# Mixer of a macaron block on one core: modulation sums tied to marked chain steps, w_out's first pieces taken into the last group's stage, sigmoid written with tanh

## The chip, the core and the metric

The kernel runs on one core of one Trainium2 chip. The metric is the device time of one execution in microseconds (us). PE is the matrix engine (PEld its weight loads), DVE the vector engine, ACT the scalar engine, POOL the GpSimd engine, and SP the engine whose queue starts most of the DMAs. Each engine works through its own instructions in order; they wait for one another by semaphores.

## The reference

One transformer block in float32 on x of 256 rows by 2048 columns. Three sublayers stand one behind the other: a SwiGLU feed-forward (ffn1), a mixer, and a second feed-forward (ffn2), each with a norm before and behind it. Nine vectors of 2048 modulate them (shift, scale and gate of each sublayer); they are c's silu times a matrix of 2048 x 18432, plus a bias.

```python
mod = (silu(c) @ w_ada + b_ada).reshape(3, 3, D)
x = x + w * (1 + gate) * rms_norm(fn(modulate(rms_norm(x, pre), shift, scale)), post)   # three times
# fn of the mixer:
p = h @ w_in                       # 512 pool columns, then r, k, v (1536 each), then 64 + 64 + 224
y_pool = multiscale_pool(p[:, :512])          # windows 2, 4, 8, 16, then a 128x128 product each
y_rwkv = rwkv7_time_mix(p[:, 512:])           # 24 heads of 64, a recurrence over the 256 rows
out = concatenate([y_pool, y_rwkv]) @ w_out
```

In rwkv7_time_mix the gate is `sigmoid(xg) @ g2`, where xg are the last 224 columns after a token shift. The recurrence carries a 64 x 64 state per head.

## The kernel before, in words

**Products.** Each weight is split into a rounded part hi (on ACT, line 185) and a rest lo (on DVE, line 186), each activation likewise, and a product is three matmuls. Line 201 issues nearly all matmuls. The dense work of the mixer comes in pieces: `dense` (line 796) makes 256 columns of w_in with two 1 MB loads and eight pieces of 12 matmuls, and yields after each; `rows_pieces` (line 588) does the same for w_out, whose pieces are six matmuls of 512 columns for one k-tile and one column block (two halves of the rows). Raw weights have two buffers, split ones four.

**Mixer.** `mixer` (line 818) begins with `outer`, which norms and modulates the input k-block by k-block and multiplies it at once with the lora columns and with r, k and v of the first head group. `lora` (line 845) then shifts the small columns; two of its three parts go through Sigmoid, the first through Tanh, and `use_ln_exp` loads the table for exp and ln behind them. Six groups of two 128-column pairs follow. A group's recurrence is done in chunks of 64 rows by two generators:

- `rwkv_a` (line 1035) has seven segments: decay and gates; the scaled keys and queries (its DVE work ends with bk, ar and wc, lines 1092 to 1103); the bonus and v; two of chunk products G; T1 and the diagonal blocks (to dg, line 1147); and the inverse of the 8 x 8 blocks, a chain of 14 small DVE steps on xt and x (lines 1166 and 1168) that ends with Z1, Z0 (the transpose of line 1175).
- `rwkv_b` (line 1178) has thirteen: four for the doubling of the inverse (pm, Z), two for its lower half (pm at line 1245, X), the corrections, three state steps S (line 1287), the output y (sq), its norm (sb<-t, the rsqrt) and the gate product (sb<-xg), which writes two k-tiles of yT.

`stage` (line 888) writes one group's order out: twelve slots; in each slot two pieces of dense work, then one segment of the old b, of b, and, in seven of the slots (0, 2, 4, 5, 6, 7, 9), of a. Each PE instruction is tied to the one before (`ordered`, line 192), so this order is PE's order until `ordered` is cleared. The dense pieces of stages 0 to 4 are the next group's r, k and v, 24 of them. Stage 5 has the 16 pieces of the pool columns, used up by slot 7; its slots 8 to 11 hold the pool's window sums and two of its four products. A last stage without a runs b of group 5, beside 24 of the 32 pieces of w_out's first two column blocks; the last k-tiles (14 and 15) come from that b, so eight pieces stand behind it. `late` (line 940) splits finished k-tiles of yT into hT, the input of w_out, whose buffer was w_in's input. Then come w_out's third and fourth column block, with `post_rows` behind each block.

**Modulation in the mixer.** `ada_run` (line 273) works off the rest of four groups of sums: vector 5, then three parts of vectors 7 and 6 (two of 2 x 256 columns, one of 2 x 512). Loads of 512 KB go into four places in x's buffer, which is saved to DRAM for that time (line 884) and read back when all is done (line 934). A load's sum is one DVE operation of 1024 elements per partition, or two of 512 (lines 255 and 257). All four groups use one accumulator tile, `acc`. When a group's 2048 rows are summed, its matmuls (`ada_mod`, line 310) and the DVE operation at line 322 follow in one of the slots 1, 3, 8, 10, 11. `stage` calls `ada_run` at the end of a slot, 0.8 times per slot while a runs; three calls only load, each group takes two calls beside its sums.

**Order on the engines other than PE.** The program gives the dependences and a priority (the order in which it is written, moved ahead for some operations), and a list scheduler fixes each engine's order before the run: an operation that is ready may be put ahead of an earlier one that isn't. `later` (line 335) ties an operation behind `self.urgent`, if that lies on its engine: the sums pass through it, and line 1028. In the mixer of before, `urgent` is last set in `outer`.

Of the kernel before, what the change touches and what calls it, by code (L numbers as in the profile page):

```python
# [11 lines left out]
F32 = mybir.dt.float32  # L12
# [5 lines left out]
P = 128  # L18
T = 256
# [13 lines left out]
ADA_FFN1, ADA_MIXER, ADA_OUT, ADA_FFN2 = 2.8, 0.8, 3, 12  # L33
# [48 lines left out]
class Block:  # L82
# [190 lines left out]
    def ada_run(self, upto, places):  # L273
# [162 lines left out]
    def post_begin(self, s, weight, more, psum, rows, junk):  # L436

        nc = self.nc
# [6 lines left out]
        ps = self.tile(psum, [P, 512], tag="mm")  # L445
        nc.tensor.transpose(ps[:KD, :P], g, self.ident)
# [137 lines left out]
    def rows_block(self, *args, **kw):  # L584
        for _ in self.rows_pieces(*args, **kw):
            pass

    def rows_pieces(self, load, nkt, per, x, banks, apart, done, more=(), warm=None, wide=1, order=None):
# [5 lines left out]
        parts = ((0, 0, 512), (1, 0, 256), (1, 256, 256)) if apart else [  # L594
            (tt, 512 * h, 512) for h in range(wide) for tt in range(2)]
        held = []

        def use(b, k0, hi, lo):
            tt, c0, n = parts[b]
            cs = slice(c0 % 512, c0 % 512 + n)  # L600
            for k in range(per):
                kt = k0 + k
                self.rows_mm(banks[b][:, :n], tt, hi[:, k, cs], lo[:, k, cs], x(kt), kt == ends[0], kt == ends[1])

        order = order or range(nkt // 4 * wide)
        ends = 4 // wide * order[0], 4 // wide * (order[-1] + 1) - 1
        for kc in order:
            raw = load(kc)
            for pc in range(0, 4 // wide, per):
                k0 = 4 // wide * kc + pc  # L610
                if wide > 1:
                    for h in range(wide):
                        hi, lo = self.split(raw[:, pc:pc + per, 512 * h:512 * h + 512])
                        for b in (2 * h, 2 * h + 1):
                            use(b, k0, hi, lo)
                        yield
                    continue
# [195 lines left out]
    def tick(self):  # L813
        self.chunks += 1
        if int(self.chunks / self.every) > int((self.chunks - 1) / self.every) and self.ada_pos < self.ada_end[ADA_AHEAD]:
            self.ada_step(self.mm)

    def mixer(self, ctx):
        nc, tc, I = self.nc, self.tc, self.I
        pool = lambda name, bufs, **kw: ctx.enter_context(tc.tile_pool(name=name, bufs=bufs, **kw))  # L820
        self.chunks, self.every = 0, ADA_MIXER
# [23 lines left out]
        def lora(i, ps):  # L845
            if i == 0:
                self.shift(xa, ps, "mu_shift", 36)
                last.append(nc.scalar.activation(xw[:C, :], xa[:C, :], AF.Tanh))
            else:
                key, j = (("mu_shift", 37), ("mu_tail", 0))[i - 1]  # L850
                t = self.tile(self.w2p, [P, T], tag="t1")
                self.shift(t, ps, key, j)
                last.append(nc.scalar.activation(xg[:, i - 1, :], t, AF.Sigmoid))
# [56 lines left out]
        us = {}  # L910

        def pool_weights():
            for h in range(2):
                yield from self.dense(w_in, h * 2 * P, 2, self.hT, lambda i, ps: us.__setitem__(2 * h + i, ps))
# [3 lines left out]
        for g in range(n):  # L918
            state[g] = {}
            a = self.rwkv_a(state[g], g, *(rkv[g, w] for w in range(3)))  # L920
            pieces = weights(g + 1) if g < n - 1 else pool_weights()
            tasks = {}
# [4 lines left out]
            stage(a, b, b_old, pieces, tasks)  # L927
            b, b_old = self.rwkv_b(g, state[g]), b
            for run in (pieces, a):
                for _ in run:  # L930
                    pass
# [3 lines left out]
        rows = self.tile(self.gp, [P, 2, 1024], tag="G")  # L935
        junk = self.tile(self.w2p, [P, 2, 512], tag="bt")
        self.post_begin(1, 1.0, True, self.mm, [rows[:, h, :] for h in range(2)], [junk[:, i, :] for i in range(2)])
        row = lambda t: self.tile(self.mm if t == "mm" else self.pa, [P, 512], tag=t)

        def late(ks):  # L940
            for k in ks:
                y = self.yT[:, k, :]
                nc.scalar.copy(self.hT[:, k, 0, :], y)
                nc.vector.tensor_tensor(self.hT[:, k, 1, :], y, self.hT[:, k, 0, :].bitcast(F32), ALU.subtract)

        self.split_ahead = 300
        self.every = ADA_OUT
        for q, tags in ((0, ("mm", "mm", "sa", "ga")), (2, ("pb", "zb")), (3, ("sb", "y", "mm"))):
            banks = [row(t) for t in tags]
            w = 2 if q == 0 else 1  # L950

            def load(kc):
                raw = self.load(I["w_out"], 4 // w * kc, 4 // w, q * 512, w * 512)
                if not self.ordered:
                    self.tick()
                return raw

            def done(tt, c0, n, ps):
                self.post_rows(q + c0 // 512, tt, c0 % 512, n, ps)
# [3 lines left out]
            order = [2, 3, 4, 5, 6, 0, 1, 7] if q == 0 else None  # L963
            pieces = self.rows_pieces(load, KD, 1, lambda k: self.hT[:, k], banks, q == 3, done, more, self.mm, w, order)
            if q == 0:
# [4 lines left out]
                for _ in b:  # L970
                    pass
                late((14, 15))
                self.ordered, self.pe_last = False, None
            for _ in pieces:
                pass

    def pool_begin(self, us):

        nc = self.nc
        self.pool_w = [self.tile(self.w2p, [P, 2, P], tag=t, bufs=1) for t in ("lw2", "la2")]  # L980
        for i, w in enumerate(self.pool_w):
            nc.sync.dma_start(w, self.I["pool_w"][2 * i:2 * i + 2].rearrange("i p c -> p i c"))
        work = self.tile(self.w2p, [P, 6 * T], tag="bk", bufs=1)
        more = self.tile(self.w2p, [P, 2 * T], tag="T1")
        n = PAD + T
        self.pool_u = work[:, :4 * n].rearrange("p (i t) -> p i t", i=4)
        self.pool_s = [work[:, 4 * n:5 * n], more[:, :n]]
        for t in [self.pool_u[:, :, :PAD]] + [s[:, :PAD] for s in self.pool_s]:
            nc.vector.memset(t, 0.0)
        for i in range(4):  # L990
# [454 lines left out]
```

## Time and profile before

| what | value |
|---|---|
| median of 3 runs | 2153.83 us (2153.71 to 2160.31) |
| the profiled execution's own time | 2149.33 us |
| its span, first to last instruction | 2147.5 us |
| mean granted clock of PE | 0.982 |
| mixer's opening, to the first a-segment | 795 to 889.9 us of the span |
| stages 0 to 5 | 889.9 to 1265.8 us |
| last stage and w_out | 1265.8 to 1372 us |

Times inside the profile count from the first instruction. A line of the timeline gives start, length, engine, line of the program, operation, output<-inputs, shape and count, and in brackets the idle time before it and what ended that. A row of a table by stretches gives from:to and length, each engine's busy time with its count of instructions, then PE's granted clock (1.00 is full), the DMA engines' busy share and GB/s. In a row of the waits stand total, number and longest. PE counts as busy while matmuls are queued one behind the other, also at half clock.

### The profile page before, as it was taken

What the parts mean: (1) busy time and instruction counts of PE and PEld (TensorE: products, weight loads), DVE (VectorE), ACT (ScalarE), POOL (GpSimd) and SP (SyncE); (2) the same over time, 40 slices, a digit from 0 to 9 for tenths busy, and PEclk for the clock granted to TensorE, in tenths of its full rate; (3) what the DMA queues carried; (4) which work ended last, traced back from release to release, by engine and by line L of the source; (5) the groups of instructions that cost most, each with busy time, mean ns of one, the idle gap of its engine ahead of it and who ended that gap; (6) DMA issues with size and microseconds to landing.
All of it is one profiled execution on the core that took longest, in us unless ns stands there. A gap on an engine that the chain in (4) does not pass through costs nothing.

```text
span 2147.5 us, 38718 instructions
## 1 busy us (share of the span) xinstructions
PE 2052.9 (96%) x15987; PEld 1825.8 (85%) x15987; DVE 1595.1 (74%) x2204; ACT 1023.3 (48%) x1503; POOL 0.2 (0%) x4
## 2 busy tenths in 40 slices
PE   3999999999999998899998999999999999999998
PEld 3999988888888887799887877899998888888886
DVE  6798898788887777777888675778899455555556
ACT  3534543444434556655444545653454344443453
POOL 0000000000000000000000000000000000000000
PEclk8999999999999998999998999999999999999999
DMA  9999888999888837843655334598887555555553
GB/s 313 359 313 329 276 284 323 313 322 319 303 325 298 284 113 242 258 124 109 180 160 190 102 105 140 212 345 284 315 296 252 196 193 181 194 182 193 194 190 124
DMA packets 313711, 506.62 MB, mean 236 GB/s; under 512 B 13013, under 2 KB 173886, under 8 KB 313022
## 3 DMA queue, kind: packets, MB, share of 16 engines
q1 hardware_dynamic: 312044, 500.78, 68.7%
q10 hardware_dynamic: 1490, 3.36, 0.5%
q8 instruction: 125, 2.05, 0.4%
q14 instruction: 52, 0.43, 0.1%
HBM read 499.87 MB, written 4.22 MB: 235 GB/s over the span
## 4 chain that ended last, share of the span: by engine, by line
PE 86%; DVE 6%; DMA 4%; ACT 3%; issue 2%; SPq 0%; DVEq 0%; ACTq 0%
PE mm L201 50%; PE mm L212 16%; PE mm L213 8%; PE sa L201 2%; PE ga L201 2%; PE zb L201 2%; DVE lo L186 2%; PE pb L201 2%; PE sb L201 2%; DVE acc L257 1%; DMA raw<-in_w_in_dram 1%; PE y L201 1%; ACT hi L185 1%; DMA x<-in_w_ada_dram 1%; DMA ada<-in_w_ada_dram 1%
## 5 line engine op out<-in xcount | busy, mean ns | idle before, releaser
L186 DVE TENSOR_TENSOR lo<-raw,hi 128x1024 fp32r<-128x1024 f32 (+2 forms) x766 | 799.0, 1050 | 399.2 <-ACT hi L185 397.1
L185 ACT CAST hi<-raw 128x1024 fp32r<-128x1024 f32 (+2 forms) x766 | 694.3, 913 | 836.2 <-PE mm L201 536.9
L201 PE MATMUL mm<-hT,hi 128*128 128x256 f32 x3648 | 675.0, 287 | 14.3 <-ACT hi L185 5.2
L201 PEld LDWEIGHTS mm<-hT,hi 128*128 128x128 f32 x3648 | 569.5, 192 | 31.9 <-issue 7.2
L212 PE MATMUL mm<-hT,hi 128*128 128x512 f32 x1536 | 539.9, 395 | 0.0
L201 PE MATMUL mm<-hT,lo 128*128 128x256 f32 x1824 | 513.6, 283 | 2.2 <-DVE lo L186 2.2
L213 PE MATMUL mm<-hT,lo 128*128 128x256 f32 x1536 | 431.8, 281 | 1.2 <-DVE lo L186 1.2
L201 PE MATMUL mm<-hi,act 128*128 128x512 f32 (+1 forms) x1312 | 398.6, 384 | 0.0
L201 PEld LDWEIGHTS mm<-hT,lo 128*128 128x128 f32 x1824 | 348.1, 191 | 3.2 <-DVE lo L186 3.2
L212 PEld LDWEIGHTS mm<-hT,hi 128*128 128x128 f32 x1536 | 288.8, 188 | 67.7
L257 DVE SCALAR_TENSOR_TENSOR acc<-ada,csilu,acc 128x1024 f32<-128x1024 f32 (+1 forms) x247 | 300.3, 1216 | 61.7 <-DMA ada<-in_w_ada_dram 59.7
L213 PEld LDWEIGHTS mm<-hT,lo 128*128 128x128 f32 x1536 | 288.0, 187 | 1.8 <-DVE lo L186 1.7
L201 PEld LDWEIGHTS mm<-hi,act 128*128 128x128 f32 x1312 | 244.3, 188 | 48.8
L201 PE MATMUL mm<-lo,act 128*128 128x512 f32 (+1 forms) x656 | 251.9, 384 | 0.0
L201 PEld LDWEIGHTS mm<-lo,act 128*128 128x128 f32 x656 | 123.3, 188 | 24.2
L670 DVE TENSOR_TENSOR act<-act,mm 128x512 f32<-128x512 f32 x96 | 64.2, 679 | 2.3 <-PE mm L201 2.0
L257 DVE SCALAR_TENSOR_TENSOR acc<-x,csilu,acc 128x512 f32<-128x512 f32 (+1 forms) x53 | 51.8, 978 | 3.0 <-DMA x<-in_w_ada_dram 2.5
L201 PE MATMUL mm<-hi,work 128*128 128x512 f32 x128 | 40.7, 389 | 0.0
L201 PE MATMUL mm<-ones,acc 128*128 128x1 f32 x96 | 13.3, 267 | 25.6 <-DVE acc L257 25.6
L201 PEld LDWEIGHTS mm<-ones,acc 128*128 128x128 f32 x96 | 13.1, 217 | 26.5 <-DVE acc L257 21.2
L668 ACT COPY act<-mm 128x512 f32<-128x512 f32 x32 | 18.8, 586 | 33.8 <-PE mm L201 33.8
L705 ACT ACTIVATE silu<-silu 128x512 f32<-128x512 f32 x24 | 15.2, 632 | 40.9 <-DVE silu L704 40.9
(365 smaller groups left out, 1695.8 us busy)
## 6 DMA issues: line engine op xcount, KB each, us to landing
raw<-in_ffn_w_down_dram SPq DMA_DIRECT2D x88, 1024.0 KB, 5.6
raw<-in_ffn_w_gate_dram SPq DMA_DIRECT2D x86, 1024.0 KB, 7.7
raw<-in_ffn_w_up_dram SPq DMA_DIRECT2D x86, 1024.0 KB, 5.2
ada<-in_w_ada_dram SPq DMA_DIRECT2D x152, 512.0 KB, 7.3
ada<-in_w_ada_dram SPq DMA_DIRECT2D x192, 256.0 KB, 4.7
raw<-in_w_in_dram SPq DMA_DIRECT2D x34, 1024.0 KB, 7.0
x<-in_w_ada_dram SPq DMA_DIRECT2D x64, 256.0 KB, 5.0
raw<-in_w_out_dram SPq DMA_DIRECT2D x16, 1024.0 KB, 5.2
```

The lines of the kernel that those rows point to most:

```text
L185: a = nc.scalar.copy(hi, raw)
L186: d = nc.vector.tensor_tensor(lo, raw, hi.bitcast(F32), ALU.subtract)
L201: return self.pe(self.nc.tensor.matmul(ps, a, b, start=start, stop=stop))
L212: nc.tensor.matmul(ps.rearrange("p a t -> p (a t)"), hi, x.rearrange("p a t -> p (a t)"), start=start, stop=False)
L213: nc.tensor.matmul(ps[:, 0, :], lo, x[:, 0, :], start=False, stop=stop)
L257: self.later(nc.vector.scalar_tensor_tensor(acc, raw[:, i], ck, acc, ALU.mult, ALU.add))
L668: nc.scalar.copy(part, bank)
L670: nc.vector.tensor_tensor(part, part, bank, ALU.add)
L705: last = nc.scalar.activation(s, s, AF.Silu)
```

## The change

- `ada_run` takes its accumulator from the pool of the 512 KB tiles (two buffers) instead of the single `acc`.
- A new `mark` sets `urgent`. Marked are, in a: the second half of ar, each G product, dg, and the transpose that makes Z0; in b: both pm products and both transposes of the doubling, X, SV and each state step S. So a sum is tied behind the operation marked last when it is written, up to its own slot's.
- In stage 5 the pool's columns are copied out of PSUM as soon as they are made, its sums stand in slots 4, 5, 8 and 9 and its products in slots 6, 7, 10 and 11; k-tiles 4 to 11 are split in slots 6 to 9. Behind the 16 w_in pieces come eight pieces of w_out (two per slot, slots 8 to 11).
- w_out's first two column blocks are read and done one at a time by quarters of k, in a written order. The last stage takes 1.5 pieces per slot, 18 in all; six are left for the time after it. Two of the six are k-tiles 12 and 13 of the second block.
- The pool's sums use other buffers; the first step of each is a copy of one column and an add of shifted columns instead of an add over a padded tile.
- The gain row of `post_begin` is made in two parts, the second in slot 4 of the last stage.
- Two of the lora parts use tanh(x/2), and a DVE operation makes 0.5 t + 0.5 of it.
- `tick` and `ADA_OUT` go; `tick` did nothing in the mixer, since all its sums were done by then.

```diff
 def ada_run
-                    self.acc = self.tile(self.accs, [P, 2, cols[0][2]], tag="acc")
+                    self.acc = self.tile(self.raws, [P, 4 * T], tag="ada", bufs=self.ada_bufs)[:, :2 * cols[0][2]]
+                    self.acc = self.acc.rearrange("p (j c) -> p j c", j=2)
...
+    def mark(self, op):
+        self.urgent = op
+        return op
...
 def lora
-                t = self.tile(self.w2p, [P, T], tag="t1")
+                t = xg[:, i - 1, :]
                 self.shift(t, ps, key, j)
-                last.append(nc.scalar.activation(xg[:, i - 1, :], t, AF.Sigmoid))
+                last.append(nc.scalar.activation(t, t, AF.Tanh, scale=0.5))
+                nc.vector.tensor_scalar(t, t, 0.5, 0.5, ALU.mult, ALU.add)
...
-        def stage(a, b, b_old, pieces, tasks):
+        def stage(a, b, b_old, pieces, rate, tasks={}):
             for s in range(SLOTS):
-                for _ in range(2):
+                for _ in range(int((s + 1) * rate) - int(s * rate)):
                     next(pieces, None)
...
+        def out_piece(q, kc):
+            if q not in banks:
+                banks[q] = [row(t) for t in (("mm", "mm"), ("sa", "ga"))[q]]
+            raw = self.load(I["w_out"], 4 * kc, 4, q * 512, 512)
+            for pc in range(4):
+                k = 4 * kc + pc
+                hi, lo = self.split(raw[:, pc:pc + 1, :])
+                for tt in range(2):
+                    self.rows_mm(banks[q][tt], tt, hi[:, 0], lo[:, 0], self.hT[:, k], k == 4, k == KD - 1)
+                yield
+
+        def last_weights():
             for h in range(2):
-                yield from self.dense(w_in, h * 2 * P, 2, self.hT, lambda i, ps: us.__setitem__(2 * h + i, ps))
+                yield from self.dense(w_in, h * 2 * P, 2, self.hT, lambda i, ps: self.pool_take(2 * h + i, ps))
+            for q, kc in ((0, 1), (0, 2), (1, 1), (1, 2), (0, 0), (1, 0), (0, 3), (1, 3)):
+                yield from out_piece(q, kc)
...
-            if g == n - 1:
-                tasks = {8: lambda: (self.pool_begin(us), self.pool_sums(0)), 9: lambda: self.pool_sums(1),
-                         10: lambda: (self.pool_out(0, "sa"), self.pool_sums(2)),
-                         11: lambda: (self.pool_out(1, "ga"), self.pool_sums(3))}
+                stage(a, b, b_old, pieces, 2, {
+                    4: lambda: self.pool_sums(0), 5: lambda: self.pool_sums(1),
+                    6: lambda: (self.pool_out(0, "y"), late(4, 5)), 7: lambda: (self.pool_out(1, "y"), late(6, 7)),
+                    8: lambda: (self.pool_sums(2), late(8, 9)), 9: lambda: (self.pool_sums(3), late(10, 11)),
+                    10: lambda: self.pool_out(2, "ga"), 11: lambda: self.pool_out(3, "ga")})
...
-            order = [2, 3, 4, 5, 6, 0, 1, 7] if q == 0 else None
-                late(range(4, 12))
-                tasks = {1: lambda: late((12, 13)), 3: lambda: self.pool_out(2, "y"), 4: lambda: self.pool_out(3, "y"),
-                         5: lambda: late(range(4))}
-                stage(None, b, b_old, pieces, tasks)
+        g_post = self.post_gain(1, 1.0)
+        stage(None, b, b_old, pieces, 1.5, {0: lambda: late(0, 1), 1: lambda: late(2, 3, 12, 13), 4: gain})
+        for _ in b:
+            pass
+        late(14, 15)
+        self.ordered, self.pe_last = False, None
+        for _ in pieces:
+            pass
+        for q in range(2):
+            for tt in range(2):
+                self.post_rows(q, tt, 0, 512, banks[q][tt])
...
 def rwkv_a
-        nc.vector.tensor_tensor(ar[:, :, 1, :], ch(r), W[:, :, 1:], ALU.mult)
+        self.mark(nc.vector.tensor_tensor(ar[:, :, 1, :], ch(r), W[:, :, 1:], ALU.mult))
...
-        nc.vector.transpose(Z0.rearrange("p u t -> p (u t)"), Z1.rearrange("p u t -> p (u t)"))
+        self.mark(nc.vector.transpose(Z0.rearrange("p u t -> p (u t)"), Z1.rearrange("p u t -> p (u t)")))
```

More of the change, by code (lines that the diff above doesn't have):

```diff
@@ L582, in rows_mm, with rows_block @@
         self.mul(ps, x[:, 1, ts], hi, False, stop)
[L584 to L595, printed above, removed]
+    def rows_block(self, load, nkt, per, x, banks, apart, done, more=(), warm=None):
+        parts = ((0, 0, 512), (1, 0, 256), (1, 256, 256)) if apart else ((0, 0, 512), (1, 0, 512))
         held = []
@@ L934, in mixer @@
         nc.sync.dma_start(flat_x, dram)
[L935 to L944, printed above, removed]
@@ L946, in mixer, with gain @@
[L946 to L948 removed]
+        def gain():
+            rows = self.tile(self.gp, [P, 2, 1024], tag="G")
+            junk = self.tile(self.w2p, [P, 2, 512], tag="bt")
+            self.post_rest(g_post, True, self.bank("y"), [rows[:, h, :] for h in range(2)],
+                           [junk[:, i, :] for i in range(2)])
+        g_post = self.post_gain(1, 1.0)
@@ L974, in mixer @@
-            for _ in pieces:
-                pass
-    def pool_begin(self, us):
-        nc = self.nc
[L980 to L990, printed above, removed]
-            nc.scalar.copy(self.pool_u[:, i, PAD:], us[i])
+            self.rows_block(load, KD, 1, lambda k: self.hT[:, k], banks, q == 3, done, more, self.mm)
```

121 lines of the change are left out of this document (62 added, 59 removed).

## The prediction

> **What bounds the kernel now.** First the page, whole run.
>
> ```profile
> span 2147.5 us, 38718 instructions
> PE 2052.9 (96%) x15987; PEld 1825.8 (85%) x15987; DVE 1595.1 (74%) x2204; ACT 1023.3 (48%) x1503; POOL 0.2 (0%) x4
> PE 86%; DVE 6%; DMA 4%; ACT 3%; issue 2%; SPq 0%; DVEq 0%; ACTq 0%
> ```
>
> PE is busy 96% of the span and carries 86% of the chain that ended last. The change takes no matmul out, so it can only win time in which PE waits or runs at half clock. I therefore read the busy times stage by stage. The columns are from:to and length, then PE, PEld, DVE, ACT and POOL busy with counts, granted clock, DMA share, GB/s. The rows are the mixer's opening up to the first a-step, the six stages g = 0 to 5 (each cut at the a-step's first matmul), and the rest up to w_out's third column block.
>
> ```profile
> 795.00:889.90 94.90, 80.40 (x543) 72.46 (x542) 71.41 (x145) 57.15 (x124) 0.00 (x0) 0.89 0.77 236
> 889.90:937.90 48.00, 46.55 (x487) 42.97 (x486) 38.58 (x77) 28.20 (x52) 0.00 (x0) 1.00 0.59 181
> 937.90:1000.25 62.35, 61.89 (x977) 55.69 (x977) 43.53 (x93) 33.73 (x63) 0.00 (x0) 1.00 0.40 116
> 1000.25:1066.66 66.41, 62.73 (x978) 56.48 (x977) 54.11 (x114) 33.62 (x63) 0.00 (x0) 1.00 0.53 155
> 1066.66:1137.18 70.52, 64.13 (x977) 57.60 (x977) 58.82 (x112) 33.73 (x63) 0.00 (x0) 0.96 0.57 175
> 1137.18:1203.17 65.99, 65.53 (x969) 58.45 (x969) 50.05 (x97) 33.95 (x63) 0.00 (x0) 0.94 0.50 155
> 1203.17:1265.80 62.63, 55.96 (x852) 47.24 (x853) 46.15 (x116) 30.76 (x63) 0.00 (x0) 0.92 0.28 92
> 1265.80:1327.30 61.50, 59.81 (x698) 46.70 (x699) 33.84 (x62) 28.18 (x52) 0.00 (x0) 1.00 0.39 125
> ```
>
> Stages 1 to 4 do the same matmuls (977 records, 969 in the last). Stage 1 needs 62.35 us; the next three need 4.06, 8.17 and 3.64 us more, together 15.9 us. A stretch of length T at mean clock c loses T x (1 - c): 2.8 us in stage 3, 4.0 us in stage 4, which is all of stage 4's excess. Now the modulation's sums, in the same stretches (DVE busy with count, then clock, DMA share and GB/s):
>
> ```profile
> L257 DVE SCALAR_TENSOR_TENSOR acc<-x,csilu,acc x53: 732/752/1284, 829.9 to 1150.0; 128x512 f32<-128x512 f32 x30, 128x1024 f32<-128x1024 f32 x23
> 937.90:1000.25 62.35, 0.00 (x0) 1.00 0.40 116
> 1000.25:1066.66 66.41, 8.96 (x12) 1.00 0.53 155
> 1066.66:1137.18 70.52, 14.34 (x13) 0.96 0.57 175
> 1137.18:1203.17 65.99, 7.06 (x6) 0.94 0.50 155
> ```
>
> The stage without sums is the fast one. How they cost time stands in the DVE timeline: the 14 small xt/x steps of the inverse, of about 0.2 us each, first in stage 1 and then in stage 3, and PE behind them.
>
> ```profile
> 985.30 0.22 DVE L1166 TENSOR_TENSOR xt<-sa,x 128x56 f32<-128x56 f32 x1 [0.39 <-PE sa L201]
> 989.95 0.45 DVE L1175 STREAM_TRANSPOSE Z<-Z 128x256 f32<-128x256 f32 x1
> 998.42 0.75 PE L201 MATMUL pb<-Z,T 32*32 32x32 f32 x64
> ...
> 1114.82 0.22 DVE L1166 TENSOR_TENSOR xt<-sa,x 128x56 f32<-128x56 f32 x1 [0.39 <-PE sa L201]
> 1130.85 1.27 DVE L257 SCALAR_TENSOR_TENSOR acc<-x,csilu,acc 128x1024 f32<-128x1024 f32 x1
> 1133.72 0.43 DVE L1175 STREAM_TRANSPOSE Z<-Z 128x256 f32<-128x256 f32 x1
> 1134.20 1.08 PE L201 MATMUL pb<-Z,T 32*32 32x32 f32 x64 [5.48 <-DVE Z L1175]
> PE pb L201 <- DVE Z L1175: 8.7, 2, 5.5
> ```
>
> In stage 1 the chain takes 4.65 us up to the transpose and PE asks for Z 8.0 us after it is there (998.42 - 990.40). In stage 3, with sums of 1.27 us between its small steps, it takes 18.9 us and PE waits 5.48 us; stage 2 has the other wait of the last row, 8.7 - 5.5 = 3.2 us. The reason is in the code: the one accumulator is free only after the modulation's matmuls in slot 8, and then every sum that is ready is queued in a burst, just where slot 9's chain stands.
>
> **The change, part by part.** *Marks and the second accumulator.* Sums now stay behind the last marked operation of their own slot, and a new group no longer waits for the matmuls of the one before. By the code's counting (0.8 per slot, held only by slot 8's modulation step) the sums fall so: stage 0 six of 1.28 us (7.7), stage 1 two of 1.28 and three pairs of 0.75 (7.1), stage 2 eight pairs (12.0), stage 3 five pairs and three of 1.28 (11.3), stage 4 twelve (15.4), stage 5 one. Slots 9 to 11 now come after Z's transpose, which is marked, so the burst inside the chain goes: minus 15.9 us. What is late next? DVE's own load: stage 1's 43.53 + 7.1 = 50.6 of 62.35 us, stage 2's 54.11 - 8.96 + 12.0 = 57.2, stage 3's 55.8, stage 4's 50.05 - 7.06 + 15.4 = 58.4, or 94%. Queued behind the held sums are the splits (lo) and the chain steps; PE waits for those. The weak place is after the marked ar operation: sums of slots 2 to 4 come free there together, in front of the step pm, on which PE already waits a little:
>
> ```profile
> PE zb L201 <- DVE pm L1245: 1.8, 4, 0.5
> ```
>
> Bounds for the new waits: 0 (the 8.0 us of slack hides them; less than 0 is excluded, because stage 1 without sums is the base), and 0.57 us per us of sum, stage 3's 8.17 / 14.34, which for the 45.8 us of stages 1 to 4 is 26 us. I take 1.5 us per stage, 6 us: stage 4 opened with nearly all of its 7.06 us of sums and lost nothing that its clock doesn't explain, so the true value is near the low end. Net of this part: -10 us.
>
> *Opening and stage 0.* The early sums leave, and their loads with them.
>
> ```profile
> x<-in_w_ada_dram SPq DMA_DIRECT2D x8, 512.0 KB
> x<-in_w_ada_dram SPq DMA_DIRECT2D x16, 256.0 KB, 5.7
> PE zb L201 <- ACT hi L185: 1.0, 2, 0.5
> PE zb L201 <- DVE lo L186: 0.8, 2, 0.6
> 870.43 1.28 ACT L848 ACT_TABLE_LOAD   x1
> 878.73 1.28 ACT L853 ACT_TABLE_LOAD   x1
> 883.85 0.79 PE L201 MATMUL mm<-hT,hi 128*128 128x256 f32 x2 [3.48 <-ACT hi L185]
> 880.20:889.90 9.70, 5.74 (x27) 5.28 (x26) 7.35 (x13) 6.61 (x14) 0.00 (x0) 0.65 0.88 278
> ```
>
> Between 820 and 890 us SP issued 8 MB of modulation weights; four places of 512 KB bound what can be fetched before the first sum, so some 6 MB move into stages 0 to 4, where the DMA share is 0.40 to 0.59. That frees w_in's loads, but PE lost only about 1.8 us to late splits there: I take 1.2. Sigmoid's table load (L853) sits in ACT's queue ahead of the split on which PE waits 3.48 us: without it 1.3 us less. The two DVE operations that tanh adds are off this path. The half clock around that wait costs 9.70 x 0.35 = 3.4 us, of which I count 1.5; stage 0 pays 0.5 for its six sums (38.58 - 2.25 + 7.7 = 44.0 of 48 us). Net -3.5 us, bounds -8 (all of these) and 0. The Trainium skill (ScalarE: Activation LUTs, Table sets: the hidden batching unit) lists tanh in sigmoid's set too; by that one load would have served both, and this edit would give 0 instead of 1.3. The trace disagrees: it has a load at each of the two lines, 8.3 us apart.
>
> *w_out earlier, pool elsewhere.*
>
> ```profile
> 1327.30:1349.70 22.40, 22.40 (x97) 17.99 (x96) 15.28 (x28) 14.38 (x31) 0.00 (x0) 1.00 0.54 181
> 1244.40:1259.20 14.80, 10.72 (x162) 7.75 (x162) 13.63 (x54) 4.26 (x10) 0.00 (x0) 0.85 0.41 143
> 1311.54 1.02 PE L201 MATMUL sb<-t,consts 128*128 128x512 f32 x2
> 1313.79 1.94 PE L201 MATMUL sb<-xg,lg 128*128 128x256 f32 x8
> 1321.62 0.50 PE L201 MATMUL mm<-hi,hT 128*128 128x512 f32 x1 [1.69 <-ACT hT L943]
> 1227.07 1.81 PE L201 MATMUL ga<-t,consts 128*128 128x512 f32 x2 [2.58 <-DVE mod L322]
> ```
>
> The first row is pure w_out: 96 matmuls in 22.40 us, 0.233 us each, so one piece (six) is 1.40 us. The second row is slots 7 to 11 of the last group's stage, where no dense work was left: 4.1 us idle and 14.80 x 0.15 = 2.2 us of clock. Eight pieces are 11.2 us; with 10.72 - 2.2 = 8.5 us of chain the stretch becomes 19.7 us, I say 20.7, and 11.2 us fall away later: -5.3. DVE there gets eight splits of 0.7 us, and one pair of pool sums goes to slots 4 and 5, so it stays at about 18 of 20.7 us. The end pays back: from sb<-t to the pieces that need the last rows were 1321.62 - 1311.54 = 10.1 us, covered by four pieces, sb<-t and sb<-xg, all but 1.69. Now only two free pieces lie behind, with 1.02 + 1.94 + 2.80 = 5.8 us of cover: the wait grows to 4.3, +2.6. Stage 5's wait on mod (2.58) keeps its place. Fewer pieces per slot (1.5) leave 2.1 us of cover for a step; I add 0.2 for one exposed step. Net -2.5 us; bounds -6.3 (both losses of the stretch, nothing back) and +4.3 (rival C). The Trainium skill (TensorE: Matmul & The Clock Gate, Why this matters for your kernels) warns of idle gaps over about 3 us, since an idle window of 3.4 us brings half clock; by it the longer wait would cost an estimated 1.7 us more. The trace has both: the clock fell after 5.48 us, not after stage 2's 3.2 us.
>
> The restore of x leaves SP's queue later, after the last sum, in stage 5 instead of stage 4. The weight loads queued behind it would be held at most a slot (62.35 / 12 = 5.2 us), and each feeds four pieces, 5.6 us: nothing. The gain row of post_begin moves to the last stage's slot 4; the 17 pieces after it (24 us) cover its two 512 KB reads, and if they didn't, post_rows and not PE would be late: nothing, or one read (5.7 us, the row of 256 KB) if that cover is gone. Pool's own matmuls and sums change place, not number, but for one small copy for each of four sums, behind DVE's other work.
>
> Sum: -10 - 3.5 - 2.5 = -16 us. The profiled execution took 2149.33 us (1.8 beside its span) and becomes 2133.3; the median of the three runs, 2153.83, lies 4.5 above it, so I predict 2138.
>
> **The rivals.** *A, slower: the held sums sit on the chains.* All 54.8 us of sums now stand directly behind chain steps. At 0.57 us per us that costs 31 us against 15.9 + 6 us won: 2163. It decides above 22 / 54.8 = 0.40. For it speaks that DVE reaches 94% in stage 4; against it stage 4's opening, with its sums and no wait.
>
> *B, the marks don't clear the chain.* A slot's own sum is held only behind slot 8's S step and may still be queued among slot 9's small steps, one or two of them instead of six. If PE's waits on Z stay, only -6 is left: 2148. Against it: 8.0 us of slack for two sums of 1.28.
>
> *C, the end gives it back.* If the two free pieces aren't moved ahead, cover is 3.0 us and the wait 7.1 instead of 1.69, +5.4; after so long a wait the clock falls, as after stage 3's 5.48 us, for which stage 4 paid 4.0. The part is then -5.3 + 5.4 + 4.0 + 0.2 = +4.3 instead of -2.5: 2144.6. For it speaks the order in the code, in which the late pieces of the first bank pair come first; against it, that PE's order is free after that point.
>
> **How the numbers follow.** The forecast has 0.60, A 0.13, B 0.12, C 0.15. A measurement can tell about 0.3% from no change, 6.5 us: faster is below 2147.4, slower above 2160.3. Faster: nearly all of the forecast, most of C and a little of B, 0.70; same, the rest of these, 0.18; slower 0.12, nearly all of A. The forecast's own range is 2125 to 2147: at one end no new waits and most of the other two bounds, at the other 12 us of new waits and half of the other two parts. The whole range takes in B, C and the mild half of A: 2125 to 2157.
>
> **What would show it.** Right: stages 1 to 4 near 64 us each, no wait of pb on Z, sums spread over all of them and none from 820 to 890, one table load less, w_out's first matmuls some 12 us before the last group's stage ends, a wait of 3 to 5 us before the last rows' pieces. Wrong: waits of zb or ga on pm, ar or G in stages 2 to 4 above 1.5 us each; stage 4 over 66 us; sums still between the xt/x steps.

## The result and the profile after

Median after 2142.35 us (2138.09 to 2145.98, 6 runs), before, on the same chip, 2155.03 us (2151.21 to 2160.31, 6 runs): ratio 0.9938 with a 95% interval of 0.9919 to 0.9957, or 12.7 us less. I had forecast 2138 and 16 us less. The profiled execution after took 2141.48 us, span 2139.7. Set against the one before (2149.33) that is only 7.9 us less, because the profiled execution before was a quick one, 5.7 us under its six-run median.

The page of the changed kernel: busy times and the chain that ended last.

```profile
PE 2050.5 (96%) x15987; PEld 1826.6 (85%) x15987; DVE 1596.0 (75%) x2209; ACT 1023.4 (48%) x1502; POOL 0.2 (0%) x4
...
PE 87%; DVE 6%; ACT 2%; DMA 2%; issue 2%; SPq 0%; DVEq 0%; ACTq 0%
```

PE's matmuls are the same 15987; the DMA share of the chain fell from 4% to 2%. Little else shows on the page, so I go by stretches. Columns as in the prediction. The rows are the opening from its first product (sa<-hT) to the first sa<-lw, stages 0 to 4, stage 5 up to its last pb<-Z, and the last stage up to w_out's third column block.

```profile
804.49:876.61 72.12, 63.95 (x484) 61.14 (x485) 41.03 (x82) 48.28 (x97) 0.00 (x0) 0.93 0.69 208
876.61:928.65 52.04, 47.93 (x488) 44.20 (x486) 43.00 (x82) 28.73 (x54) 0.00 (x0) 0.96 0.62 185
928.65:994.02 65.37, 64.92 (x978) 57.78 (x977) 51.71 (x105) 33.88 (x63) 0.00 (x0) 0.95 0.49 146
994.02:1059.19 65.17, 62.64 (x981) 56.44 (x977) 55.74 (x114) 33.84 (x63) 0.00 (x0) 1.00 0.58 168
1059.19:1124.35 65.16, 62.63 (x980) 56.44 (x976) 54.95 (x111) 33.85 (x63) 0.00 (x0) 1.00 0.58 173
1124.35:1188.87 64.52, 61.82 (x973) 55.55 (x969) 59.17 (x110) 33.67 (x63) 0.00 (x0) 1.00 0.60 186
1188.87:1253.60 64.73, 61.88 (x834) 52.55 (x830) 52.33 (x123) 36.76 (x74) 0.00 (x0) 1.00 0.39 129
1253.60:1313.53 59.93, 53.89 (x719) 41.84 (x719) 31.17 (x59) 22.94 (x45) 0.00 (x0) 0.91 0.35 120
```

Before, the opening measured in the same way is this row (of the kernel before, same view):

```profile
806.31:889.72 83.41, 69.85 (x484) 65.06 (x485) 62.20 (x105) 50.10 (x99) 0.00 (x0) 0.88 0.85 259
```

Put side by side, each part from such marks in the two profiles:

| part | before | after | change | my term |
|---|---|---|---|---|
| up to the mixer's first product | 806.31 | 804.49 | -1.8 | 0 |
| opening | 83.41 | 72.12 | -11.3 | -4.0 |
| stage 0 | 48.09 | 52.04 | +4.0 | +0.5 |
| stage 1 | 62.37 | 65.37 | +3.0 | in the next row |
| stages 2 to 4 | 202.92 | 194.85 | -8.1 | -10 (stages 1 to 4) |
| stage 5 and last stage, to the third column block | 124.22 | 124.66 | +0.4 | -2.5 |
| rest (w_out's end, ffn2) | 820.2 | 826.2 | +6.0 | 0 |

Up to w_out's third column block the change is worth 13.8 us. The rest is unchanged code; over all the profiles of this study it took 820.2 to 828.8 us, and kernels whose code there is that of before stand at both 820.2 and 826.1. I count its +6.0 as variation between executions.

PE's waits in the mixer of the changed kernel (sum, number, longest):

```profile
PE zb L201 <- DVE pm L1255: 7.8, 4, 2.5
PE mm L201 <- ACT hT L907: 4.0, 1, 4.0
PE pb L201 <- DVE Z L1185: 3.2, 1, 3.2
...
PE ga L201 <- DVE mod L323: 2.9, 1, 2.9
...
PE pb L201 <- DVE X L1261: 2.0, 1, 2.0
```

The two waits on Z of stages 2 and 3 (8.7 us together) are gone: no sum lies among the xt/x steps any more. In stage 3 the chain that took 18.9 us up to Z's transpose now takes 4.65 (DVE's timeline):

```profile
1109.47 0.22 DVE L1176 TENSOR_TENSOR xt<-sa,x 128x56 f32<-128x56 f32 x1 [0.39 <-PE sa L201]
...
1114.12 0.45 DVE L1185 STREAM_TRANSPOSE Z<-Z 128x256 f32<-128x256 f32 x1
```

In place of the two waits stand a wait on pm in each of stages 2 to 4, one on Z in stage 0, one on X in the last stage, and the longer one on hT. The sums (DVE busy with count, clock, DMA share, GB/s) lie where I had put them:

```profile
804.49:876.61 72.12, 0.00 (x0) 0.93 0.69 208
876.61:928.65 52.04, 7.36 (x6) 0.96 0.62 185
928.65:994.02 65.37, 6.44 (x8) 0.95 0.49 146
994.02:1059.19 65.17, 11.19 (x15) 1.00 0.58 168
...
1124.35:1188.87 64.52, 15.28 (x12) 1.00 0.60 186
```

So the size was about right and the parts were not: the opening gave three times its term, the stages together gave 1.1 us where I had 9.5, the end gave nothing.

### The profile page after: what moved, and what is told of

Its sections match the earlier page's. It is cut to its first block, busy times and chain, and to the rows that moved or that the text cites. A ratio compares the mean times of both kernels' runs of the same rounds, so it can differ in the third digit from the quotient of the medians.

```text
span 2139.7 us, 38742 instructions
## 1 busy us (share of the span) xinstructions
PE 2050.5 (96%) x15987; PEld 1826.6 (85%) x15987; DVE 1596.0 (75%) x2209; ACT 1023.4 (48%) x1502; POOL 0.2 (0%) x4
## 4 chain that ended last, share of the span: by engine, by line
PE 87%; DVE 6%; ACT 2%; DMA 2%; issue 2%; SPq 0%; DVEq 0%; ACTq 0%
PE mm L201 51%; PE mm L212 17%; PE mm L213 8%; PE zb L201 2%; PE sa L201 2%; PE ga L201 2%; DVE lo L186 2%; PE sb L201 2%; PE pb L201 2%; DVE acc L257 1%; DMA raw<-in_w_in_dram 1%; PE y L201 1%; ACT hi L185 1%; DMA ada<-in_w_ada_dram 0%; DVE act L668 0%
## 5 line engine op out<-in xcount | busy, mean ns | idle before, releaser
L257 DVE SCALAR_TENSOR_TENSOR ada<-x,csilu,ada 128x512 f32<-128x512 f32 (+1 forms) x45 | 41.5, 922 | 0.2
L201 PE MATMUL mm<-hi,hT 128*128 128x512 f32 (+1 forms) x88 | 30.9, 407 | 4.0 <-ACT hT L907 4.0
```

What stands on the lines that cost most here:

```text
L201: return self.pe(self.nc.tensor.matmul(ps, a, b, start=start, stop=stop))
L257: self.later(nc.vector.scalar_tensor_tensor(acc, raw[:, i], ck, acc, ALU.mult, ALU.add))
```

## The experiments

My theory after the result: (1) the opening is shorter because the 20 early sums left DVE, not because of transfers; (2) the waits on pm are sums in front of pm; (3) stage 0's wait on Z has another cause than the sums' time on DVE; (4) starting w_out early gains nothing as written. Rivals stand in the expectations. Each ratio is to the kernel before run beside it on the same chip; lengths come from one profile each, between the same marks. A length can differ by some 3 us between executions through the clock alone: the changed kernel and the one with w_out late have the same code up to stage 4 and the same three waits on pm within 0.01 us, but stages 2 to 4 took 194.85 us in one profile and 197.84 in the other, where stages 3 and 4 ran at a clock of 0.97.

| kernel | median us (runs) | ratio to before, 95% | opening | stage 0 | stage 1 | stages 2 to 4 | last part |
|---|---|---|---|---|---|---|---|
| before | 2155.03 (6) | | 83.41 | 48.09 | 62.37 | 202.92 | 124.22 |
| after | 2142.35 (6) | 0.9938, 0.9919 to 0.9957 | 72.12 | 52.04 | 65.37 | 194.85 | 124.66 |
| tanh alone | 2155.23 (10) | 0.9984, 0.9969 to 0.9999 | 81.23 | 47.62 | 62.39 | 203.90 | 124.24 |
| marks alone | 2149.15 (9) | 0.9963, 0.9941 to 0.9984 | 73.34 | 51.40 | 66.43 | 199.28 | 124.32 |
| after, marks do nothing | 2164.47 (10) | 1.0033, 1.0018 to 1.0048 | 82.46 | 59.83 | 66.48 | 200.04 | 127.54 |
| after, w_out late | 2140.09 (4) | 0.9898, 0.9857 to 0.9938 | 71.40 | 51.81 | 65.29 | 197.84 | 123.28 |
| before, thin loads | 2157.57 (1) | | 81.07 | 47.70 | 62.41 | 206.62 | 126.13 |
| after, thin loads | 2139.76 (1) | | 70.90 | 48.76 | 62.39 | 200.57 | 124.69 |
| after, ar unmarked | 2140.83 (10) | 0.9938, 0.9918 to 0.9958 | 71.37 | 51.60 | 66.39 | 199.21 | 124.92 |
| after, no sums in stage 0 | 2140.55 (4) | 0.9932, 0.9909 to 0.9954 | 72.34 | 47.54 | 65.92 | 197.81 | 121.65 |
| after, none in slots 2, 3 | 2130.51 (6) | 0.9882, 0.9860 to 0.9903 | 71.06 | 51.66 | 66.70 | 188.94 | 121.88 |
| the same, w_out late | 2126.46 (5) | 0.9856, 0.9831 to 0.9880 | 70.59 | 51.33 | 65.44 | 188.94 | 118.40 |
| none in slots 2, 3 nor late in stage 0 | 2132.68 (6) | 0.9884, 0.9862 to 0.9906 | 73.40 | 47.55 | 65.50 | 188.87 | 123.83 |
| after, 1.25 pieces per slot | 2133.60 (4) | 0.9887, 0.9860 to 0.9914 | 72.14 | 50.72 | 62.39 | 196.35 | 119.74 |

**The parts alone.** Tanh without the rest, and the marks with the second accumulator without the rest (the edits are those parts of the change's diff).

> The kernel before with only the sigmoid edit. Opening (mixer's first matmul to stage 0's first a-matmul): 83.6 us before, 72.1 after. Theory (the opening's gain comes from the sums and their loads leaving it): 82 us, one table load of 1.28 us and at most its share of the half clock less; all later stages as before (48.0, 62.4, 66.4, 70.5, 66.0), median -1 to -3 us. Rival (the table load on ACT's queue was what held the opening): 77 us or less, median -6 us or more.

> The kernel before with only the marks and the accumulator in two buffers; w_out, pool and sigmoid as before. Theory: opening 73 to 75 us (sums and 6 MB of loads gone from it, Sigmoid's table load still there); stages 2 to 4 near 65 us each with a wait of about 2.5 us of zb on pm in each (0.5 before) and none of pb on Z there; the rest from stage 5 on as before (124.2), so median -11 to -14 us: nearly the whole gain of the change. Rival (the parts need each other; the gain lies in the w_out and pool edit): median within 5 us of before.

Tanh alone took its table load away. The wait at the opening's end went from 3.48 to 3.08 us only, and PE's idle time in the whole opening (length less busy) stayed at 13.5 us; the 2.2 us are clock (0.92 against 0.88), which the kernel before with thin loads, below, has as well. Beside the marks, tanh does more: that wait is 1.84 us with marks alone and 0.91 in the changed kernel, 0.91 to 1.27 over all profiles that have both. The marks alone bring 10.1 of the opening's 11.3 us; this is its row:

```profile
807.31:880.65 73.34, 64.04 (x485) 61.12 (x485) 40.73 (x80) 49.66 (x98) 0.00 (x0) 0.93 0.68 204
```

Their stages 2 to 4 are only 3.6 us shorter, with the same three waits on pm and clocks of 0.97. The ratio of 0.9963 is about 8 us, less than the 11 to 14 that I had expected.

**Marks that do nothing.**

```diff
     def mark(self, op):
-        self.urgent = op
         return op
```

> The changed kernel, except that marking an operation does nothing; the second accumulator buffer, w_out, pool and tanh stay. Theory: the sums run ahead again, as early as the four places and two accumulators let them: opening 80 to 83 us, bursts in stages 0 to 3, waits of pb on Z of 3 us or more in at least one stage; median 5 to 12 us above the changed kernel. Rival (the second accumulator alone dissolves the bursts, the marks do nothing): same time as the changed kernel within 3 us, and no burst among the xt/x steps.

The sums of this kernel, opening and stages 0 to 2:

```profile
806.19:888.65 82.46, 19.22 (x20) 0.90 0.85 259
888.65:948.48 59.83, 13.42 (x18) 0.90 0.71 229
948.48:1014.96 66.48, 0.00 (x0) 0.93 0.34 101
1014.96:1086.04 71.08, 11.93 (x10) 0.96 0.55 164
```

It is about 20 us over the changed kernel (0.0095 of 2155), more than the 5 to 12 that I expected, and slower than before: with two accumulators and no marks the sums run as early as they can, 20 in the opening and 18 in stage 0, and PE waits 4.08 us on ar, 4.73 and 5.48 on Z. Without the marks nothing of the gain is left. The second accumulator without any other part was not run.

**Transfers or DVE?** The mixer's modulation loads are cut to 32 of 128 partitions, in the kernel before and in the changed one; the sums keep their size.

```diff
     def ada_load(self, cols, kk, per, place=None):
         width = cols[0][2]
+        n = P if place is None else 32
...
-            self.nc.sync.dma_start(raw.rearrange("p k j c -> p k (j c)"), w[:, :, ...])
+            self.nc.sync.dma_start(raw[:n].rearrange("p k j c -> p k (j c)"), w[:n, :, ...])
...
```

> The kernel before, with the mixer's modulation loads cut to 32 of 128 partitions (three quarters of these weights are not read, so the modulation is not the reference's; the sums run unchanged over whatever the places hold). Two theories for the opening, which took 83.4 us before and 73.3 with marks alone. Transfers: w_in's loads came late because 8 MB of modulation weights were in the same queue and on the same DMA engines; then the opening falls to 74 to 77 although the 20 sums are still in it. VectorE: the 20 sums (19.2 us) held the splits; then it stays at 82 to 84. The bursts in stages 2 and 3 are sums, so by both theories their waits on Z (3.2 and 5.5 us) and lengths (66.4 and 70.5) stay.

> The changed kernel with the same cut of the mixer's modulation loads to 32 of 128 partitions (modulation not the reference's, sums unchanged). Transfers theory for stage 0: the wait of 3.20 us on Z comes from a w_in load that landed 2.98 us late beside two modulation loads; it goes to under 1, stage 0 falls from 52.0 to 48 to 49, and stage 1, no longer at half clock, from 65.4 to 62.4 to 63.5. Rival: the held sums on VectorE make it; then the wait stays at 3 us and stage 0 at 52. The waits on pm in stages 2 to 4 (2.53, 2.53, 2.26) come from sums on VectorE and stay by both; if they go too, they were transfers as well.

The opening of the kernel before with thin loads, and then stages 0 and 1 of the changed kernel with thin loads (one execution each):

```profile
805.77:886.84 81.07, 67.17 (x484) 62.44 (x485) 62.01 (x105) 49.99 (x99) 0.00 (x0) 0.92 0.66 190
```

```profile
874.90:923.66 48.76, 46.78 (x489) 43.12 (x487) 41.79 (x81) 28.82 (x54) 0.00 (x0) 1.00 0.53 159
923.66:986.05 62.39, 61.93 (x980) 55.75 (x977) 52.87 (x106) 33.76 (x63) 0.00 (x0) 1.00 0.43 123
```

In the opening PE's idle time is 81.07 - 67.17 = 13.9 us with thin loads, 13.6 with full ones, and 9.3 with marks alone, where loads and sums are gone. So the transfers cost PE no waiting there, and DVE's 19.2 us of sums cost 4.3 us of it. PE's busy time for the same matmuls falls by 5.8 us (69.85 to 64.04); half clock accounts for most of that, 83.41 x 0.12 = 10.0 us against 73.34 x 0.07 = 5.1. Not all of it need be the sums' doing: with all 20 sums in place the busy time was 67.17 us with thin loads and 67.70 with tanh alone, so 3.1 to 5.8 us of it went with the marks. In stage 0 it is the other way round: with thin loads the wait on Z falls from 3.20 to 1.1 us, stage 0 is 3.3 us shorter, and stage 1 is back at 62.39 and full clock. That full clock may be chance: the kernel with 1.25 pieces per slot has it too, behind a wait of 3.00 us. The timeline of the changed kernel shows the chain:

```profile
914.01 0.34 SPq L244 DMA_DIRECT2D x<-in_w_ada_dram  x1
915.22 0.37 SPq L175 DMA_DIRECT2D raw<-in_w_in_dram  x1
916.41 0.34 SPq L244 DMA_DIRECT2D x<-in_w_ada_dram  x1
...
923.60 0.62 ACT L185 CAST hi<-raw 128x512 fp32r<-128x512 f32 x1 [2.98 <-DMA raw<-in_w_in_dram]
924.25 0.69 DVE L186 TENSOR_TENSOR lo<-raw,hi 128x512 fp32r<-128x512 f32 x1 [2.06 <-ACT hi L185]
...
925.26 0.43 DVE L1185 STREAM_TRANSPOSE Z<-Z 128x256 f32<-128x256 f32 x1
...
925.75 1.08 PE L201 MATMUL pb<-Z,T 32*32 32x32 f32 x64 [3.20 <-DVE Z L1185]
```

A weight load goes out between two modulation loads, whose places the held sums have just freed. Its split waits 2.98 us for it, the lo waits for the split, and Z's transpose, whose input was ready at 922.2, stands behind that lo. The Trainium skill (Perfetto Trace Analysis, Tensor Engine Instruction) says that DVE and ACT are strict FIFOs; the trace agrees: the transpose didn't pass a lo that stood for 2.06 us.

**What the sums in front of pm stand behind.**

```diff
-        self.mark(nc.vector.tensor_tensor(ar[:, :, 1, :], ch(r), W[:, :, 1:], ALU.mult))
+        nc.vector.tensor_tensor(ar[:, :, 1, :], ch(r), W[:, :, 1:], ALU.mult)
```

> The changed kernel with the ar operation no longer marked, so that the sums of slots 2 to 4 come free at an earlier mark. Theory: the sums freed behind ar stand between ar and pm; the three waits on pm fall from 2.5 to about 0.5 each, stages 2 to 4 go from 65.2, 65.2, 64.5 to 62.5 to 63.5 each, and the time falls by 4 to 6 us against the changed kernel (near 2137). Rival: the sums then stand before another step of the chains (X, the transposes, or ar itself), which PE waits for instead: the wait moves and the time stays within 2 us.

The place in stage 2, first in the changed kernel, then with ar unmarked (timelines):

```profile
1015.52 0.44 DVE L1243 STREAM_TRANSPOSE Z<-Z 128x256 f32<-128x256 f32 x1
...
1016.45 0.68 DVE L1109 TENSOR_TENSOR ar<-y,W 128x512 f32<-128x512 f32 x1
1017.04 0.75 DVE L257 SCALAR_TENSOR_TENSOR ada<-x,csilu,ada 128x512 f32<-128x512 f32 x1
...
1018.53 0.74 DVE L257 SCALAR_TENSOR_TENSOR ada<-x,csilu,ada 128x512 f32<-128x512 f32 x1
1019.39 0.69 DVE L186 TENSOR_TENSOR lo<-raw,hi 128x512 fp32r<-128x512 f32 x1
...
1020.72 0.43 DVE L1255 COPY pm<-pb 32x256 f32<-32x256 f32 x1
...
1021.29 0.69 PE L201 MATMUL zb<-Z,pm 32*32 32x32 f32 x32 [2.53 <-DVE pm L1255]
```

```profile
1020.88 0.43 DVE L1243 STREAM_TRANSPOSE Z<-Z 128x256 f32<-128x256 f32 x1
...
1022.41 0.74 DVE L257 SCALAR_TENSOR_TENSOR ada<-x,csilu,ada 128x512 f32<-128x512 f32 x1
...
1023.68 0.74 DVE L257 SCALAR_TENSOR_TENSOR ada<-x,csilu,ada 128x512 f32<-128x512 f32 x1
...
1025.71 0.43 DVE L1255 COPY pm<-pb 32x256 f32<-32x256 f32 x1
...
1026.29 0.79 PE L201 MATMUL zb<-Z,pm 32*32 32x32 f32 x32 [2.53 <-DVE pm L1255]
```

Here my theory fell as I had put it: the waits stay at 2.53, 2.53 and 2.12 us, and so does the ratio. Without ar's mark two sums stand in the same place, behind the transpose of Z, which is marked too. Two sums of 0.75 us and one more lo (0.6) make the 2.07 us by which the wait exceeds the 0.46 of before.

**No sums in those slots, or none in stage 0.** The condition in `stage` gets `and s not in (2, 3)`; in the other kernel `and slots > SLOTS`.

> The changed kernel with no modulation load or sum before stage 1; from there one in every slot until the count has caught up, so that stages 1 to 4 take the six sums of stage 0 (7.4 us) as well. Theory: stage 0 loses its wait on Z and falls to 48.0 as before the change; stage 1 keeps full clock, 62.4 to 63.5; together 6 to 7 us less; stages 2 to 4 keep their waits on pm, 65 each. Rival: the six sums cost as much where they go (0.57 us per us, 4 us, or a first wait in stage 1), so that 0 to 3 us are left.

> The changed kernel with no modulation step in slots 2 and 3 of a stage; the count catches up at one per slot in the other ten. With ar unmarked the wait on pm had stayed at 2.53, because the two sums then came free behind the transpose of Z just ahead and stood in the same place. Theory: it is these two sums of 0.75 us, with one more split, between the second transpose of Z and pm, whatever frees them; without them pm comes as early as in stage 1 (wait 0.45), stages 2 to 4 go from 65 to 62.4 to 63.5 each, and the time falls by 5 to 8 us against the changed kernel (2133 to 2137). Rival: VectorE's load is the limit (51 to 59 of 65 us busy); then other waits of PE (on G, Z or lo) take the place and the time stays within 2 us.

Stages 2 to 4 of the kernel without sums in slots 2 and 3:

```profile
991.90:1055.02 63.12, 62.66 (x981) 56.48 (x977) 55.47 (x114) 33.90 (x63) 0.00 (x0) 1.00 0.60 174
1055.02:1118.12 63.10, 62.64 (x981) 56.46 (x977) 54.70 (x111) 33.91 (x63) 0.00 (x0) 1.00 0.59 178
1118.12:1180.84 62.72, 61.82 (x973) 55.56 (x969) 56.75 (x108) 33.67 (x63) 0.00 (x0) 1.00 0.61 189
```

The three waits are gone and no other came in these stages: 5.9 us, with DVE as busy as before (55 to 57 us of 63). The mod wait of stage 5 (2.85) went too, since that modulation now comes later. It is place and not load that counted. Without sums in stage 0 the wait on Z went as well (47.54 us), but the sums, now one in each slot of stage 1, met pm there: a wait of 2.27 us, stage 1 at 65.92, and no gain left. The rival was right there.

**Both, and w_out late.** The condition excludes slots 2 and 3 and slots 6 to 11 of stage 0.

> The changed kernel with no modulation step in slots 2 and 3 of any stage and none in the second half of stage 0, so that no modulation load goes out beside stage 1's weights, and the sums move to slots 4 to 11 of stages 1 to 4 and into stage 5. Theory: stage 0 48 us (52.0 in the changed kernel), stage 1 at full clock 62.4 to 63.5 (65.4), stages 2 to 4 62.4 to 63.5 each: 8 to 13 us less than the changed kernel, 2129 to 2134. Rival: the five or six sums that are then queued between X and Z's transpose in the second half of a stage, with nine where there were six, make a wait on G or Z of 2 us or more in stages 2 and 3, and 4 to 6 us are given back.

Stages 0 to 4 are the shortest of all, 301.9 us against 307.3 without the second exclusion. But stage 1 didn't come down to 62.4: a new wait of 2.35 us (ga<-sums on the DVE operation at line 307) stands in it. The time is no better (0.9884 against 0.9882): in this profile the opening took 2.3 us more at a clock of 0.91 (0.98 in the other), and the last part, with three more sums in stage 5, 1.9 us more. What of that belongs to this kernel and what to the one execution I can't say.

**w_out's start and the last stage's rate.** Late: w_out starts only in the last stage.

```diff
+            yield from [None] * 8
             for q, kc in ((0, 1), (0, 2), (1, 1), (1, 2), (0, 0), (1, 0), (0, 3), (1, 3)):
...
-        stage(None, b, b_old, pieces, 1.5, {0: ...
+        stage(None, b, b_old, pieces, 2, {0: ...
```

> The changed kernel with w_out not begun in the last group's stage: its slots 8 to 11 hold no dense piece, the last stage takes two pieces per slot and eight remain behind it, as before; pool's places, marks and tanh stay. Last part (stage 5's first a-matmul to w_out's third column block): 124.2 us before, 124.7 after. Theory (the early pieces won some 9 us in stage 5 and lost as much in the last stage by thin cover: X 2.0, hT 4.0 and 5 us of half clock): within 2 us of 124.7, with the wait on hT back to 2 us or less and no wait on X, and stage 5 idle in its last four slots. Rival (the early pieces are worth their 5 us and other edits of that part, pool above all, ate it): 129 us or more.

> The kernel before this one, with w_out also begun only in the last stage as in the run with the late w_out. Theory: the early start of w_out brings nothing (the stretch from the last group's stage to the third column block was 124.2 us before, 124.7 with it and 123.3 without it), so that this takes 0 to 3 us less than without sums in slots 2 and 3 alone. Rival: the early start is worth the 2.5 us that I forecast for it, and this is that much slower.

> The changed kernel with 1.25 instead of 1.5 pieces of w_out per slot in the last stage, so that 15 pieces and not 18 lie in it and 5 instead of 2 that don't need the last rows lie behind it. Theory: cover for the wait on the last rows grows by 3 x 1.40 us, and the wait of 4.01 goes to 0 to 0.5; the slots with only one piece show one or two waits more (X, now 2.03); net 1 to 3 us less in the stretch from stage 5 to the third column block (124.7). Rival: what is taken out of the slots leaves the chain bare there, and the stretch stays within 1 us.

Late is no worse on the changed kernel (last part 123.28 against 124.66) and 3.5 us better without sums in slots 2 and 3 (118.40 against 121.88); 1.4 us of the 3.5 are idle time of PE, the rest is busy time at a clock of 0.99 against 0.96. The wait on hT fell to 1.51 us as expected, but the one on X, which I had expected to go, stayed at 1.98. But with 1.25 instead of 1.5 pieces per slot and w_out still early, the last part is 119.74. In the changed kernel's last stage (timeline), and then all of PE's listed waits from stage 5 on with 1.25:

```profile
1273.46 0.62 ACT L185 CAST hi<-raw 128x512 fp32r<-128x512 f32 x1 [1.60 <-PE mm L201]
...
1274.12 0.69 DVE L186 TENSOR_TENSOR lo<-raw,hi 128x512 fp32r<-128x512 f32 x1 [1.52 <-ACT hi L185]
1274.84 0.42 DVE L1261 COPY X<-zb 32x256 f32<-32x256 f32 x1
1275.40 1.15 PE L201 MATMUL pb<-rhs,X 64*64 64x64 f32 x32 [2.03 <-DVE X L1261]
...
1305.53 0.80 PE L201 MATMUL mm<-hi,hT 128*128 128x512 f32 x1 [4.01 <-ACT hT L907]
```

```profile
PE ga L201 <- DVE mod L323: 2.9, 1, 2.9
PE zb L201 <- issue: 0.2, 1, 0.2
```

With 1.25 both waits are gone, on X too, which I had not expected: at 1.5 the lo of a later piece, which waits until PE frees a split, stands ahead of X on DVE. The last stage is then at full clock (1.00 against 0.91), but stage 5 is not (0.92 against 1.00), and over the whole part the clock is 0.96 in both. What is won is PE's idle time, 3.3 us against 8.9.

The kernel without sums in slots 2 and 3 and with w_out late beats both the kernel before and the changed one: 2126.46 us (2120.28 to 2130.19), ratio 0.9856 (0.9831 to 0.9880) to before. Its lead over the same kernel with w_out early (0.9882, 0.9860 to 0.9903) is not clear of the noise. Slots 2 and 3 free together with the rate of 1.25 was not tried.

## Why the prediction was right or wrong

The forecast (faster; 2138, measured 2142.35) held, and none of the three rivals came. A was met in mild form only: sums on chains cost 5.9 us of idle time in stages 2 to 4, not 31. B didn't happen: PE's waits on Z in stages 2 and 3 are gone. Nor did C: the wait was 4.01 us, not 7.1, though the clock did fall to 0.91 in the last stage.

*Marks: minus 15.9, plus 6.* The waits on Z in stages 2 and 3 went, as said. The new waits came at pm in stages 2 to 4, the weak place that I had named, and cost 5.9 us of idle time against the 6 that I took: about 2 in each of three stages, not 1.5 in each of four. Excess over 62.35 us fell from 15.9 to 7.8 there. That it fell so far is in part luck: in the profile with w_out late, with the same code and waits there, it fell only to 10.8, because stages 3 and 4 ran at 0.97. The reason was half right: the sums stand between a transpose of Z and pm, and ar's mark is not needed for that. My own test, waits above 1.5 us each, called this wrong, and the place it named is what the best version mends.

*Opening: minus 4.0, measured 11.3.* The failed step is "PE lost only about 1.8 us to late splits there: I take 1.2". I counted two lines of the waits (lo and hi before zb) and read the early sums by their loads. The marks alone brought 10.1 us, 4.3 of idle time and 5.8 of busy time, mostly half clock; with the loads alone cut, the idle time didn't fall. The bound of 8 was too low because it held the same two lines; nor do the terms named for it (1.8, 1.3 and 3.4) add up to more than 6.5. Tanh's 1.3 us measured 0.6 to 0.9 beside the marks and 0.4 alone. The Trainium skill (ScalarE: Activation LUTs, Table sets: the hidden batching unit) lists tanh in sigmoid's set and in exp's as well; my reading of it, by which one load would have served tanh and sigmoid, is again not borne out: the trace of tanh alone has two loads, that of before three.

*Stage 0: plus 0.5, measured 4.0, and 3.0 more in stage 1.* The failed step is that I followed SP's queue only for the restore of x and for what the loads' absence frees. I had 6 MB of loads moved into stages with a DMA share of 0.40 to 0.59 and let them cost nothing. One of them, sent out beside a weight load, cost a late split, a wait of 3.2 us on Z and then half clock in stage 1, as in six of the seven profiles with a wait of 3.0 to 3.7 us there.

*w_out: minus 2.5, measured plus 0.4.* The wait on hT came out as worked (4.01; 4.3 forecast). The first failed step is "I add 0.2 for one exposed step": the wait on X was 2.03 us. The second is that I put all of the stretch's 5.3 us to w_out's pieces. Before, PE stood idle for 3.26 us in slots 7 to 11 in front of the pool's first product there (sa<-bk,lw); with w_out late that wait is gone too, so the pool's new places took it away and not w_out. Half clock was no gain either: 0.92 in stage 5 before, 0.91 in the last stage after (59.93 x 0.09 = 5.4 us), 0.96 over the part both times. With 1.25 pieces per slot, where the waits on hT and X are gone, the part is 3.5 us shorter than with w_out late and 4.5 shorter than before. So an early start at the lower rate is worth about 3.5 us; as written, the longer wait on hT (4.01 us, 1.51 with w_out late) and the one on X stood against it.

The sum was near because the errors, -7.3 us in the opening, +8.4 in the stages and +2.9 in the last part, nearly cancel. That is luck.

## What to carry to other kernels

When filler work is tied behind chain steps, the places that are left free count as much as the tying (here 0.9938 became 0.9882): look for the chain step that PE needs next after each mark, and leave those slots empty. To price filler on an in-order engine, count the idle time and the half clock of the whole stretch in which it lies, not the waits that bear its name. If a transfer is freed by the work that moves, follow its queue to the next weight load.

## What the runs showed of the hardware

The price of a wait in half clock is not fixed by its length. Stage 0's wait on Z was 3.00 us with 1.25 pieces per slot and stage 1 behind it ran at 1.00; it was 2.97 us with w_out late and stage 1 ran at 0.95, some 3 us longer. The waits of 2.53 us on pm left stages 2 and 3 at 1.00 in the changed kernel and at 0.97 with marks alone, 1.5 us longer each; with w_out late the same wait left stage 2 at 1.00 and stage 3 at 0.97. The Trainium skill (TensorE: Matmul & The Clock Gate, What's actually happening) says that the window of 3.4 us over which activity is judged is free-running. If so, it would matter where in it a gap falls; these pairs agree with that, and no run here shows the window itself.
